# Modulation vectors in pairs over four blocks of partitions, their steps tied to the work around them, and the first head's gates by halves

## The chip, the cores and the metric

The kernel runs on one core of a Trainium2 chip. The core has a matrix engine (TensorE, PE in the profile; its weight loads are PEld), a vector engine (VectorE, DVE), an activation engine (ScalarE, ACT), a general engine (GpSimd, POOL) and a queue that here only issues DMAs (SyncE, SP). Each engine takes its instructions in order, and semaphores tie them together. The metric is the time of one execution on the device in microseconds (us). The runs before gave a median of 2446.35 us (three runs, 2445.74 to 2447.03).

## The reference

A trunk of two layers works on x (1 x 1024 x 1024, float32). Layer 0 mixes tokens with forgetting attention (16 heads of 64), layer 1 with gated linear attention (GLA, 4 heads, a recurrence over chunks); after each comes a SwiGLU channel mixer (hidden width 2816). Every sub-layer is normalised and modulated by six vectors that come from a conditioning vector c:

```python
c_act = jax.nn.silu(c)
for i in range(DEPTH):
    mod = c_act @ ada_w[i] + ada_b[i]              # 1024 x 6144 per layer
    sh1, sc1, g1, sh2, sc2, g2 = jnp.split(mod, N_MOD, axis=-1)
    h = modulate(rms_norm(x, norm1_g[i]), sh1, sc1)
    y = forgetting_attention(h, ...) if i % 2 == 0 else gated_linear_attention(h, ...)
    x = x + g1 * y
    h = modulate(rms_norm(x, norm2_g[i]), sh2, sc2)
    x = x + g2 * swiglu(h, ffn_w_in[i], ffn_w_out[i])
return rms_norm(x, final_g)
```

The gates of GLA are log_sigmoid of a low-rank projection, summed along the chunk: `b = cumsum(log_sigmoid(a @ w_a2 + b_a) / 16)`, and q and k are scaled by exp(b), exp(-b) and exp(b_last - b).

## The kernel before, in words

Activations lie transposed: 128 features by 1024 tokens per tile, in halves of 512 tokens. A product in float32 is made of three matmuls (`mm3`, L237 to L239) of operands that were split in a high and a low part: ACT writes the high part (L159, or L202 for weights), DVE or POOL the low part (L160, L205). SP loads the weights through a ring of three raw buffers (`wr`, `load_w`, L194).

The order of instructions on each engine is not simply the order in the program: a planner, which runs a model of the engines, picks the next instruction of each engine among those that it believes ready, earlier ones in the program first. It can move an instruction ahead of others where it believes its engine idle. `tc.issue_after(ins)` forbids it, for instructions of the same engine as `ins`, to come before `ins`; it adds no semaphore.

The stages on the chip are: loads, modulation vectors 0 and 1 of layer 0 and the first projections (to about 105 us); attention of layer 0 interleaved with the projections of the next pair of heads (`weave`; to about 640); the channel mixer of layer 0 (to about 1320); GLA (to about 1700); the channel mixer of layer 1 and the final norm.

A modulation vector is a matrix times a vector, and the kernel computes it without the matrix engine's streaming: 128 rows of `ada_w` are loaded at a time, multiplied by their eight values of silu(c) (`cact`, one value per partition) and added up in `acc`; at the end the 128 partitions are summed by matmuls with a column of ones, one per 128 columns (L377, tile `mp`), and the bias is added (L379, `modc`). `ada_steps` (L336) is a generator of such steps, and two paces, `ada0` and `ada1`, run it a step at a time beside other work:

- In attention (vectors 2 to 5 of layer 0) a step loads 128 x 1024 into a buffer of `wr` (`ada`, L345), and DVE does both operations in four instructions of 256 columns (L367, L369). Each projection of a pair of heads is worth three steps.
- In the channel mixer of layer 0 (vectors 0 and 1 of layer 1, `mid0`) and in GLA (vectors 2 to 5 of layer 1) a step loads 128 x 512 into one of three, in GLA of two buffers (`ad`, L345). ACT multiplies (L358 the first, L360 the others) and POOL adds (L361). `ADA_A` and `ADA_B` are what the two parts of a step cost the pace; every product of the mixer (`prod`) and every projection of GLA pays into it.

`ada0_mod` (L462 to L473), which makes vectors 0 and 1 of layer 0 at the start from tiles `adas` with its own `acc`, is not touched. `first_evac` ends the first projections.

In GLA the first head begins with `gv_body` (values, two blocks of 128 tokens each), `a_body` (the low-rank projection, one half of the tokens) and `gate_z` (L1596 to L1599). `gate_sum` (L1605 to L1610) does exp and ln on ACT, a subtraction and two scans on DVE, on tiles `b16` and `t2` (`b_s` and `t_s` in the rows). `gate_exps` (L1635 to L1642) makes all exponentials. `head_front` then projects K (`gk`) and Q (`gqp`), evacuates them with those exponentials, and steps `gate_ahead`, which makes the gates of the next head. `mp`, `gk`, `gqp`, `z` and `gv` share a ring of three PSUM banks (`pj`).

Of the kernel before, what the change touches and what calls it, by code (L numbers as in the profile page):

```python
# [9 lines left out]
F32 = mybir.dt.float32  # L10
# [4 lines left out]
ALU = mybir.AluOpType  # L15
# [38 lines left out]
def trunk(ctx, tc, x, c, ada_w, ada_b, norm1_g, norm2_g, ffn_w_in, ffn_w_out,  # L54
# [99 lines left out]
    nc.vector.memset(mhalf, -0.5)  # L154
    maskb = cst.tile([P, P], BF16, name="maskb")
# [130 lines left out]

    load_x(0)
# [28 lines left out]
    nc.scalar.activation(cact, vps[:, P:P + 8], AF.Silu)  # L316
    nc.vector.tensor_copy(vec, vps)
# [18 lines left out]
    def ada_steps(l, j, acc_of, raw_of, w):  # L336

        steps = deque((c0, k) for c0 in range(0, D, w) for k in range(8))
        got = deque()

        def load():
            if steps:
                c0, k = steps.popleft()
                raw = raw_of([P, w], F32, f"ada{l}{j}{c0}{k}")
                nc.sync.dma_start(raw, ada_w[l, psl(k), j * D + c0:j * D + c0 + w])  # L345
                got.append(raw)

        for c0 in range(0, D, w):
            acc = acc_of([P, w], F32, f"acc{l}{j}{c0}")
            for k in range(8):  # L350
                if w == D or c0 == k == 0:
                    load()
                raw = got.popleft()
                if w < D:
                    load()
                    yield ADA_A
                    if k == 0:
                        nc.scalar.mul(acc, raw, cact[:, 0:1])  # L358
                    else:
                        nc.scalar.mul(raw, raw, cact[:, k:k + 1])  # L360
                        nc.gpsimd.tensor_add(acc, acc, raw)  # L361
                    yield ADA_B
                    continue
                for q in range(0, w, 256):
                    cs = slice(q, q + 256)
                    if k == 0:
                        nc.vector.tensor_scalar(acc[:, cs], raw[:, cs], cact[:, 0:1], None, op0=ALU.mult)  # L367
                    else:
                        nc.vector.scalar_tensor_tensor(acc[:, cs], raw[:, cs], cact[:, k:k + 1], acc[:, cs],  # L369
                                                       op0=ALU.mult, op1=ALU.add)  # L370
                yield 1.0
            if w < D:
                yield ADA_B
            n, b = w // P, c0 // P
            mp = pj([P, n], F32, f"mp{l}{j}{c0}")
            for k in range(n):
                nc.tensor.matmul(mp[:, k:k + 1], acc[:, psl(k)], ones, start=True, stop=True)  # L377
            o = l * 48 + j * 8 + b
            nc.vector.tensor_add(modc[:, l, j, b:b + n], mp, vec[:, o:o + n])  # L379
            for i, jj in ((0, 1), (1, 4)):  # L380
                if j == jj:
                    make_a(l, i, slice(b, b + n))
        yield 1.0
# [25 lines left out]
    def ada1_queue(js, acc, raws_, w):  # L409
        r = Cycle(raws_)  # L410
        for j in js:
            ada1.q.append(ada_steps(1, j, lambda *_: acc, r, w))
# [441 lines left out]
    first_evac(1, acc)  # L854
    def v_half(g, half):
# [135 lines left out]
    for j in (2, 3, 4, 5):  # L991
        ada0.q.append(ada_steps(0, j, acc_r, wr, D))
# [523 lines left out]
    def mid0():  # L1516
        v = Views(slots["hid"], 2, [HALF], "ad0").v
        ada1_queue((0, 1), v[0], v[1:4], HALF)
# [24 lines left out]
    ada1_queue((2, 3, 4, 5), ada_v[0], ada_v[1:3], HALF)  # L1543
    ADA_A, ADA_B = 2.5, 1.0
# [57 lines left out]
    def gate_sum(h, bt):  # L1602

        b16, t2 = bt
        nc.scalar.activation(t2, t2, AF.Exp, scale=-1.0)  # L1605
# [311 lines left out]
```

## Time and profile before

| what | us |
|---|---|
| median of three runs | 2446.35 |
| the profiled execution | 2444.76 |
| its span, first to last instruction | 2443.0 |
| PE busy | 2384.9 |
| PEld busy | 2028.7 |
| DVE busy | 1703.0 |
| ACT busy | 1192.8 |
| POOL busy | 1151.1 |

The time of an execution is the span and 1.76 us around it. In the rows of the profile stand a line of the kernel, an engine, an operation, and what it writes and reads by the program's names; `x96` is a count. In lists of groups the next numbers are busy time in us, mean ns of one, and the idle time before it with what ended it. In lists of waits they are us in total, times, and the longest. In the timeline a row begins with the start and the duration in us, and square brackets hold the idle time of the engine before it and what ended it. Matmuls overlap, so a row of them lasts longer than the step to the next. PEclk is the clock granted to PE, as a share of full speed.

### The profile page before, as it was taken

The numbers are of one execution on the slowest core, as the hardware profiler recorded it, in microseconds if no ns is written. First come the engines' busy times: TensorE is split into PE (matmuls) and PEld (weight loads), VectorE is DVE, ScalarE is ACT, GpSimd is POOL, SyncE is SP. The second block draws the span as 40 slices with busy tenths as digits, with TensorE's granted clock in tenths as the row PEclk, the third lists the DMA queues.
The fourth block names the chain that finished last, engine by engine and source line by source line (L and its number), as shares of the span: only waits on it lengthen the run. The fifth ranks groups of instructions, "written<-read, shape, count | busy, mean of one in ns | idle before, by whom it ended". The sixth has DMA issues, their size and how long they took to land.

```text
span 2443.0 us, 35539 instructions
## 1 busy us (share of the span) xinstructions
PE 2384.9 (98%) x12458; PEld 2028.7 (83%) x12458; DVE 1703.0 (70%) x2849; ACT 1192.8 (49%) x2280; POOL 1151.1 (47%) x1006
## 2 busy tenths in 40 slices
PE   6999999999999999999999899999999999999998
PEld 5788888878887878888888798898888888888888
DVE  6477777776687768675788456546487667665787
ACT  4565665665554443435324756654344333335325
POOL 4233333333348776653363544442326656653362
PEclk9999999999999999999999999999999999999999
DMA  8224333233326544347665333435325434347664
GB/s 269 80 87 121 96 96 120 70 96 113 128 94 212 183 164 164 125 162 261 228 215 178 92 114 111 125 107 169 107 73 191 147 134 155 130 166 257 232 209 149
DMA packets 319067, 362.34 MB, mean 148 GB/s; under 512 B 18140, under 2 KB 246648, under 8 KB 318888
## 3 DMA queue, kind: packets, MB, share of 16 engines
q1 hardware_dynamic: 318888, 360.07, 44.2%
q8 instruction: 98, 1.61, 0.3%
q14 instruction: 81, 0.66, 0.1%
HBM read 269.76 MB, written 90.24 MB: 147 GB/s over the span
## 4 chain that ended last, share of the span: by engine, by line
PE 82%; DVE 7%; DMA 3%; ACT 3%; issue 3%; POOL 2%; SPq 0%; DVEq 0%; POOLq 0%; ACTq 0%
PE p_b L237 15%; PE p_b L239 15%; PE p_b L238 14%; PE o_b L947 2%; PE t_b L933 2%; PE qk_b L237 2%; PE qk_b L238 2%; PE qk_b L239 2%; DMA ad_s<-in_ada_w_dram 1%; PE s_b L902 1%; PE s_b L903 1%; PE gv_b L237 1%; PE gv_b L239 1%; PE gv_b L238 1%; PE vps_b L237 1%
## 5 line engine op out<-in xcount | busy, mean ns | idle before, releaser
L160 DVE TENSOR_TENSOR o_s<-xv_s,o_s 128x512 fp32r<-128x512 f32 (+1 forms) x376 | 325.8, 870 | 90.3 <-ACT o_s L159 89.0
L159 ACT CAST o_s<-xv_s 128x512 fp32r<-128x512 f32 (+1 forms) x376 | 217.3, 586 | 307.2 <-PE p_b L239 257.7
L237 PE MATMUL p_b<-B,o_s 128*128 128x512 f32 x608 | 236.9, 392 | 6.5 <-DVE x L1285 4.1
L238 PE MATMUL p_b<-B,o_s 128*128 128x512 f32 x608 | 238.1, 392 | 0.0
L239 PE MATMUL p_b<-B,o_s 128*128 128x512 f32 x608 | 237.5, 391 | 0.0
L913 POOL TENSOR_SCALAR lp_s<-lp_s,st 128x128 f32<-128x128 f32 (+7 forms) x128 | 96.2, 756 | 294.2 <-DVE st L912 280.8
L683 POOL TENSOR_TENSOR ex_s<-xv_s,xv_s 128x512 f32<-128x512 f32 (+1 forms) x64 | 89.3, 1396 | 254.2 <-DMA xv_s<-in_ffn_w_in_dram 92.1
L237 PE MATMUL p_b<-T,o_s 128*128 128x512 f32 x480 | 187.4, 391 | 0.0
L238 PE MATMUL p_b<-T,o_s 128*128 128x512 f32 x480 | 186.8, 389 | 0.0
L239 PE MATMUL p_b<-T,o_s 128*128 128x512 f32 x480 | 182.0, 389 | 0.0
L237 PEld LDWEIGHTS p_b<-B,o_s 128*128 128x128 f32 x608 | 114.9, 189 | 31.6 <-DVE x L1285 3.4
L239 PEld LDWEIGHTS p_b<-B,o_s 128*128 128x128 f32 x608 | 114.9, 189 | 24.0
L238 PEld LDWEIGHTS p_b<-B,o_s 128*128 128x128 f32 x608 | 114.9, 189 | 23.7
L911 ACT ACTIVATE lp_s<-lp_s,st 128x128 f32<-128x128 f32 (+7 forms) x128 | 99.3, 776 | 56.4 <-DVE st L907 55.9
L1285 DVE TENSOR_TENSOR ex_s<-ex_s,p_b 128x512 f32<-128x512 f32 x140 | 94.0, 681 | 34.6 <-PE p_b L239 34.3
L159 ACT CAST pt_s<-t_b 128x512 fp32r<-128x512 f32 (+1 forms) x160 | 80.1, 547 | 71.5 <-PE t_b L933 70.5
L685 POOL TENSOR_TENSOR xv_s<-ex_s,xv_s 128x512 f32<-128x512 f32 (+1 forms) x64 | 84.0, 1312 | 62.5 <-DVE o_s L160 60.4
L160 DVE TENSOR_TENSOR pt_s<-t_b,pt_s 128x512 fp32r<-128x512 f32 (+1 forms) x160 | 96.5, 631 | 18.2 <-ACT pt_s L159 17.5
L239 PEld LDWEIGHTS p_b<-T,o_s 128*128 128x128 f32 x480 | 90.1, 188 | 18.9
L238 PEld LDWEIGHTS p_b<-T,o_s 128*128 128x128 f32 x480 | 90.1, 188 | 18.5
L237 PEld LDWEIGHTS p_b<-T,o_s 128*128 128x128 f32 x480 | 90.1, 188 | 18.5
L907 DVE CUSTOM_DVE_ANT_0 lp_s<-s_b,cum_s 128x512 f32<-128x512 f32 (+3 forms) x128 | 72.7, 570 | 41.7 <-PE t_b L933 22.9
(1947 smaller groups left out, 7543.4 us busy)
## 6 DMA issues: line engine op xcount, KB each, us to landing
xv_s<-in_ffn_w_in_dram SPq DMA_DIRECT2D x176, 256.0 KB, 3.0
hid_B<-x SPq DMA_DIRECT2D x70, 512.0 KB, 2.6
ad_s<-in_ada_w_dram SPq DMA_DIRECT2D x96, 256.0 KB, 2.9
hid_T<-x SPq DMA_DIRECT2D x36, 512.0 KB, 2.7
xv_s<-in_ffn_w_out_dram SPq DMA_DIRECT2D x96, 192.0 KB, 4.6
ada_s<-in_ada_w_dram SPq DMA_DIRECT2D x32, 512.0 KB, 3.8
xv_s<-in_ffn_w_out_dram SPq DMA_DIRECT2D x40, 256.0 KB, 2.8
T2o<-hid_T SPq DMA_DIRECT2D x18, 512.0 KB, 8.5
```

The costliest lines, as they stand in the source:

```text
L159: nc.scalar.copy(hi, src)
L160: nc.vector.tensor_sub(lo, src, hi.bitcast(F32))
L237: nc.tensor.matmul(ps, ah, bh, start=start, stop=False)
L238: nc.tensor.matmul(ps, ah, bl, start=False, stop=False)
L239: nc.tensor.matmul(ps, al, bh, start=False, stop=stop)
L683: nc.gpsimd.tensor_add(s1, a21, a22)
L685: nc.gpsimd.tensor_sub(a11, s1, a11)
L907: nc.vector.tensor_tensor_reduce(lp[:, k0:k1], ps, cm[:, k0:k1], 1.0, mcur, ALU.add, ALU.min, mnew)
L911: nc.scalar.activation(lp, lp, AF.Exp, bias=mcur, scale=-1.0, accum_out=st[:, qi, 2:3])
L913: nc.gpsimd.tensor_scalar(lp, lp, st[:, qi, 3:4], 1.0, op0=ALU.mult, op1=ALU.mult)
L933: nc.tensor.transpose(tp[:, i, :], lps[qi][:, psl(2 * b + jj)], ident)
L1285: nc.vector.tensor_add(d, d if src is None else dest(G, src), ps)
```

## The change

Two vectors are made together. The 1024 rows of `ada_w` are taken as 32 groups r of 32 rows s. A step s loads row 32 r + s of each group r, over the 2048 columns of two vectors, with the columns cut in four blocks of 512: partition 32 q + r holds block q of group r. Each step is therefore still 128 x 512, but comes as four DMAs (32 partitions each), and `acc` is one tile of 512 columns for both vectors. In attention a buffer holds two steps. `cblk` holds silu(c) laid out for it (loaded four times, on ACT's queue, at the start), and `quart` has a 1 in column q for the partitions of block q, so that one matmul per 128 columns gives four sums. A pair has 32 steps of 128 x 512 (or 16 of two), as two vectors had before.

The DVE instructions of layer 0's steps may not come before the last DVE instruction of the first projections (`held`). The ACT multiplications of layer 1's steps may not come before the last ACT instruction written before them (`ADA_LAG` 0, in the channel mixer) or the seventh last (`ADA_LAG` 6, in GLA). In the first head of GLA sums and exponentials of the gates are made by halves of the tokens, the first half before the third value block, and the first head steps `gate_ahead` after its Q halves instead of its K halves.

```diff
+    quart = cst.tile([P, 4], F32, name="quart")
+    nc.vector.memset(quart, 0.0)
+    for q in range(4):
+        nc.vector.memset(quart[32 * q:32 * q + 32, q:q + 1], 1.0)
...
+    craw = mrows[4][:, 0:32]
+    cblk = cst.tile([P, 32], F32, name="cblk")
+    for q in range(4):
+        nc.scalar.dma_start(craw[32 * q:32 * q + 32], c[0].rearrange("(r s) -> r s", s=32))
...
+    nc.scalar.activation(cblk, craw, AF.Silu)
...
-    def ada_steps(l, j, acc_of, raw_of, w):
+    def last_of(e, n=0):
+        return [i for i in nc.cur_bb.bb.instructions[-400:] if i.engine == ENG[e]][-1 - n]
+
+    ADA_LAG = 0
+
+    def ada_pair(l, j, acc_of, raw_of, n):
+
+        steps = deque(range(0, 32, n))
+        got = deque()
+        rows_ = ada_w[l, :, j * D:(j + 2) * D].rearrange("(r s) (q m) -> q r s m", s=32, q=4)
 
         def load():
             if steps:
+                s = steps.popleft()
+                raw = raw_of([P, n * HALF], F32, f"ada{l}{j}{s}")
+                for q in range(4):
+                    nc.sync.dma_start(raw[32 * q:32 * q + 32].rearrange("r (s m) -> r s m", s=n),
+                                      rows_[q, :, s:s + n])
+                got.append((s, raw))
+
+        acc = acc_of([P, HALF], F32, f"acc{l}{j}")
+        for i in range(0, 32, n):
+            if n > 1 or i == 0:
+                load()
+            s0, raw = got.popleft()
+            if n == 1:
+                load()
+                yield ADA_A
+                with tc.issue_after(last_of("A", ADA_LAG)):
+                    if i == 0:
+                        nc.scalar.mul(acc, raw, cblk[:, 0:1])
                     else:
+                        nc.scalar.mul(raw, raw, cblk[:, i:i + 1])
+                if i:
+                    nc.gpsimd.tensor_add(acc, acc, raw)
                 yield ADA_B
+                continue
+            tie = held[0]
+            for s in range(s0, s0 + n):
+                for c0 in range(0, HALF, 256):
+                    cs, rs_ = slice(c0, c0 + 256), slice((s - s0) * HALF + c0, (s - s0) * HALF + c0 + 256)
+                    with tc.issue_after(tie):
+                        if s == 0:
+                            nc.vector.tensor_scalar(acc[:, cs], raw[:, rs_], cblk[:, 0:1], None, op0=ALU.mult)
+                        else:
+                            nc.vector.scalar_tensor_tensor(acc[:, cs], raw[:, rs_], cblk[:, s:s + 1], acc[:, cs],
+                                                           op0=ALU.mult, op1=ALU.add)
+            yield 1.0
+        if n == 1:
+            yield ADA_B
+        mp = pj([P, 16], F32, f"mp{l}{j}")
+        for b in range(4):
+            nc.tensor.matmul(mp[:, b:16:4], acc[:, psl(b)], quart, start=True, stop=True)
+        o = l * 48 + j * 8
+        nc.vector.tensor_add(modc[:, l, j:j + 2, :].rearrange("p j k -> p (j k)"), mp, vec[:, o:o + 16])
+        if j in (0, 4):
+            make_a(l, j // 4)
         yield 1.0
...
     first_evac(1, acc)
+    held = [last_of("D")]
...
-    for j in (2, 3, 4, 5):
-        ada0.q.append(ada_steps(0, j, acc_r, wr, D))
+    for j in (2, 4):
+        ada0.q.append(ada_pair(0, j, acc_r, wr, 2))
...
-        ada1_queue((0, 1), v[0], v[1:4], HALF)
+        ada1_queue((0,), v[0], v[1:4])
...
-    ada1_queue((2, 3, 4, 5), ada_v[0], ada_v[1:3], HALF)
-    ADA_A, ADA_B = 2.5, 1.0
+    ada1_queue((2, 4), ada_v[0], ada_v[1:3])
+    ADA_A, ADA_B, ADA_LAG = 2.5, 1.0, 6
...
-    def gate_sum(h, bt):
+    def gate_sum(h, bt, halves=(0, 1)):
 
         b16, t2 = bt
...
+        w = slice(halves[0] * HALF, (halves[-1] + 1) * HALF)
+        nc.scalar.activation(t2[:, w], t2[:, w], AF.Exp, scale=-1.0)
+        nc.scalar.activation(t2[:, w], t2[:, w], AF.Ln, bias=1.0)
+        nc.vector.tensor_sub(t2[:, w], b16[:, w], t2[:, w])
+        for hf in halves:
...
-    def gate_exps(h, bt):
+    def gate_exps(h, bt, halves=(0, 1), to=None):
...
-            next(ahead, None)
+            if h:
+                next(ahead, None)
         wq = feed.next()
...
+            if not h:
+                next(ahead, None)
         return kin, qt
...
+    to0 = sm.tile([P, 4, NB], F32, tag="dec", name="dec0"), Tr([P, S], F32, "ei0")
+    gate_sum(0, bt, (0,))
+    gate_exps(0, bt, (0,), to0)
     vt.append(gv_body(0, wv, 2))
     a_body(aw, 1, bt)
     gate_z(0, (1,), bt)
-    gate_sum(0, bt)
-    b16, t2, ei, dec = gate_exps(0, bt)
+    gate_sum(0, bt, (1,))
+    b16, t2, ei, dec = gate_exps(0, bt, (1,), to0)
     vt.append(gv_body(0, wv, 3))
```

More of the change, by code (lines that the diff above doesn't have):

```diff
@@ L341, in load @@
         def load():
             if steps:
[L343 to L358, printed above, removed]
-                    else:
[L360 to L372, printed above, removed]
-                yield ADA_B
[L374 to L382, printed above, removed]
```

27 lines of the change are left out of this document (13 added, 14 removed).

## The prediction

> **What bounds the kernel now.** I read the page's totals first, then the list of what PE waited for, then busy time by stretch, and last the order of instructions where PE stands still. On the page:
>
> ```profile
> span 2443.0 us, 35539 instructions
> PE 2384.9 (98%) x12458; PEld 2028.7 (83%) x12458; DVE 1703.0 (70%) x2849; ACT 1192.8 (49%) x2280; POOL 1151.1 (47%) x1006
> PE 82%; DVE 7%; DMA 3%; ACT 3%; issue 3%; POOL 2%; SPq 0%; DVEq 0%; POOLq 0%; ACTq 0%
> ```
>
> PE is busy all but 58.1 us, and the chain that ended last is PE for 82%. So only two things shorten this kernel: fewer TensorE instructions, or fewer of those 58.1 us. The waits of PE and the busy time by stretch (columns: stretch, its length, then PE, PEld, DVE, ACT and POOL busy, granted clock, DMA) say where they lie:
>
> ```profile
> PE mp_b L472 <- DVE acc L470: 6.6, 2, 5.3
> PE gk_b L237 <- DVE modc L379: 4.6, 1, 4.6
> 63.30:68.80 5.50, 4.63 (x18) 3.94 (x19) 2.35 (x7) 3.96 (x7) 2.27 (x3) 0.50 0.72 223
> 1388.90:1393.20 4.30, 4.30 (x10) 3.43 (x11) 2.17 (x6) 4.18 (x15) 0.00 (x0) 0.50 0.00 1
> 711.00:1240.00 529.00, 522.49 (x2317) 431.98 (x2316) 381.72 (x484) 224.19 (x397) 325.82 (x224) 1.00 0.55 193
> 1824.00:2330.00 506.00, 506.00 (x2234) 419.00 (x2233) 353.93 (x464) 201.56 (x356) 272.45 (x189) 1.00 0.51 178
> ```
>
> A stall is paid twice: after each of the two long ones PE works on at granted clock 0.50. The channel mixer of layer 0, which carries modulation steps of layer 1, loses 6.5 us of PE; that of layer 1, without them, loses none.
>
> **The change part by part.**
>
> *Matmuls removed.* One modulation vector needed 8 matmuls with the accumulator as weights; a pair of vectors now needs 4.
>
> ```profile
> L377 PE MATMUL mp_b<-ones,ad_s 128*128 128x1 f32 x96 | 11.7, 233 | 0.0
> L377 PE MATMUL mp_b<-ones,acc_s 128*128 128x1 f32 x64 | 8.2, 236 | 0.0
> 753.07 0.39 PE L239 MATMUL p_b<-B,o_s 128*128 128x512 f32 x1
> 753.30 0.50 PE L377 MATMUL mp_b<-ones,ad_s 128*128 128x1 f32 x4
> 753.66 0.49 PE L237 MATMUL p_b<-T,o_s 128*128 128x512 f32 x1
> 753.99 0.40 PE L238 MATMUL p_b<-T,o_s 128*128 128x512 f32 x1
> ```
>
> The trace shows two records for each of these f32 matmuls: 160 for 10 vectors of 8. After it 5 pairs of 4 leave 40, so 120 go. By busy time a record is 19.9/160 = 0.124 us, 14.9 in all. By what they push away: from 753.30 to 753.99 are 0.69 us, of which the ordinary step of 0.23 (753.07 to 753.30) belongs to the next matmul; 0.46 for 4 records is 0.115 each, 13.8 in all; without the change-over, 0.36/4 = 0.09, 10.8. PE has no idle time there to absorb it. I take the middle, **-13.0** (-10.8 to -14.9). Four moving columns instead of one, and one addition of 16 columns on DVE instead of two of 8 or four of 4, I cost at nothing: the first is beside a full weight load, the second off the path; were that cover gone, the fewer additions would still be a gain.
>
> *Held back at first.* Layer 0's first accumulation steps now may not pass the last DVE instruction of the first projections. DVE, then PE, today:
>
> ```profile
> 56.57 1.21 DVE L367 TENSOR_SCALAR acc_s<-ada_s,cact 128x256 f32<-128x256 f32 x1
> 57.70 1.33 DVE L470 SCALAR_TENSOR_TENSOR acc<-adas_s,cact,acc 128x256 f32<-128x256 f32 x1
> 58.95 3.20 DVE L367 TENSOR_SCALAR acc_s<-ada_s,cact 128x256 f32<-128x256 f32 x3
> 62.07 0.68 DVE L484 TENSOR_TENSOR h0l<-y_s,h0h 128x512 fp32r<-128x512 f32 x1
> 63.29 0.98 PE L472 MATMUL mp_b<-ones,acc 128*128 128x1 f32 x4 [5.28 <-DVE acc L470]
> ```
>
> Four instructions of L367, whose vectors only the output projection after attention needs, stand ahead of the last two L470 (one at 57.70, one behind 62.07) that PE waits for: 1.13 + 3.12 = 4.25 us of start-to-start time. They go; a neighbour may get slower, so -3.8. Then the half clock: 5.5 us at 0.50 cost 2.75, of which I take half, -1.4, since about 1.5 us of stall stay. Sum **-5.2** (-3.0 to -7.0). The Trainium skill, "TensorE: Matmul & The Clock Gate", Part 1, says that the rate is set by whole windows of about 3.4 us; the two 0.50 rows above agree that the slow time outlasts the stall. By that rule a stall well under a window would give back all 2.75, and the sum would be 1.35 lower.
>
> What the hold costs: the steps keep their buffers longer, and SP, in order, waits with the next weight loads for them.
>
> ```profile
> 64.76 0.38 SPq L194 DMA_DIRECT2D wv_s<-in_fox_w_in_dram  x1
> 105.94 4.93 POOL L205 TENSOR_TENSOR wv_0l_s<-wv_s,wv_0h_s 128x256 fp32r<-128x256 f32 x3 [12.88 <-ACT wv_0h_s L202]
> 121.14 0.28 PE L237 MATMUL vps_b<-wv_0h_s,h0h 128*128 128x256 f32 x1
> ```
>
> The weights are split 41 us after their issue and used by PE at 121, so most of the delay is slack; 0 to +5, nearer 0: **+1.0**. The 16 postponed DVE instructions then run beside attention, where DVE has room.
>
> *First head's gates by halves.* Today, ACT, then DVE, then PE (another table load, as long, stands between the two):
>
> ```profile
> 1379.47 1.28 ACT L1605 ACT_TABLE_LOAD   x1
> 1380.77 1.06 ACT L1605 ACTIVATE t_s<-t_s 128x1024 f32<-128x1024 f32 x1
> ...
> 1383.14 1.06 ACT L1606 ACTIVATE t_s<-t_s 128x1024 f32<-128x1024 f32 x1
> 1384.23 1.23 DVE L1607 TENSOR_TENSOR t_s<-b_s,t_s 128x1024 f32<-128x1024 f32 x1 [3.77 <-ACT t_s L1606]
> 1385.49 3.28 DVE L1610 TENSOR_TENSOR_SCAN b_s<-ad_s,t_s 128x512 f32<-128x512 f32 x2
> 1388.88 0.79 PE L237 MATMUL gk_b<-h1h,w_h_s 128*128 128x512 f32 x1 [4.62 <-DVE modc L379]
> ```
>
> PE's 4.6 us end at 1388.88, when DVE has evacuated `mp`, which sat behind that chain on DVE and held the bank PE wanted. Two causes go: there are 2 `mp` instead of 8 in this stage, none after the first K projection, and half of the chain is done earlier (half of 1.06 twice, of 1.23 and of 3.28: 3.3 us). `next(ahead)` of the first head moves behind its Q projections, so its `z` no longer takes a bank between the K projections. Price: the first half adds about two table loads, 2 x 1.28 = 2.6 us, to an ACT that waits in this stretch. -4.6, and the half clock of 1388.90:1393.20, 4.3/2 = 2.1: **-6.7** (0 if another evacuation takes its place, -6.7 at best; nearest the row itself).
>
> *Steps tied.* An ACT multiplication of a step may no longer be moved ahead of the ACT work written before it (six instructions of grace in the recurrence). Today it is moved ahead and then waits for its DMA, with weight splits queued behind it:
>
> ```profile
> ACT ad_s L360 <- DMA ad_s<-in_ada_w_dram: 83.7, 55, 5.6
> SPq L345 <- POOL ad_s L361: 135.0, 71, 9.0
> L345 SPq DMA_DIRECT2D ad_s<-in_ada_w_dram x96: 327/328/532, 709.9 to 1649.8; - x96
> L361 POOL TENSOR_TENSOR ad_s<-ad_s,ad_s x51: 1277/1298/2212, 719.0 to 1654.1; 128x512 f32<-128x512 f32 x51
> L360 ACT ACTIVATE ad_s<-ad_s,cact x84: 707/724/729, 717.6 to 1653.0; 128x512 f32<-128x512 f32 x84
> DMA to landing us min/median/max: 2.6/2.9/5.7
> ```
>
> It can return the 6.5 us of 711 to 1240, or move them: behind a later multiplication wait POOL's addition, POOL's weight sums, and SP's next load. +3 to -6.5; I take **-2.5**, under half. The additions become 93 instead of 84: 9 x 1.30 = 11.7 us of POOL, hidden by its idle 203 us of 711:1240 and by the recurrence.
>
> *Quarter loads.* A step's 256 KB come as 4 issues, so 288 more in layer 1 and, by the same count, 96 in layer 0: 384 x 0.328 = 126 us of SP. SP is on the ending chain with 0%, and a load is issued a step ahead of its use; I cost it at **0** (-0 to +126: the rival below). A step lands about 3 x 0.33 = 1.0 us later.
>
> *At the start* four small loads on ACT's queue, a second Silu and five small fills. On SP such an issue took 0.36, so 1.4 us; ACT waited 2.09 us for x:
>
> ```profile
> 1.24 0.36 SPq L290 DMA_DIRECT2D mrows_s<-in_c_dram  x1
> ...
> 4.17 1.06 ACT L439 ACTIVATE sq_s<-xt_s 128x1024 bf16<-128x1024 f32 x1 [2.09 <-DMA xt_s<-in_x_dram]
> 4.88 0.28 PE L312 MATMUL vps_b<-ident,mrows_s 32*128 32x32 f32 x1 [4.88 <-DMA mrows_s<-in_final_g_dram]
> ```
>
> Hidden, but they share the DMA engines with x: 0 to +1.4, **+0.4**.
>
> Sum: -13.0 - 5.2 + 1.0 - 6.7 - 2.5 + 0 + 0.4 = -26.0. The profiled execution took 2444.76 us (span 2443.0 and 1.76 around it), so 2418.8; the median shown, 2446.35, is 1.6 above it: **2420**.
>
> **The rivals.**
>
> *The stalls come back elsewhere.* An order made anew puts new short waits where the old ones were; only the matmuls go: 2446.35 - 13.0 = 2433. For it: the planner moved those instructions ahead because it believed DMA and POOL faster than they are, and it still will. Against: both long stalls have one named instruction that the change takes out of the way.
>
> *It does nothing measurable.* If PE's time between those matmuls were set by others, the 13 us would turn into waiting: 2446. Against: idle 0.0 in both L377 rows.
>
> *Slower: SP's queue.* SP issues in order, and 135 us of it already wait at L345 for POOL's additions; behind the four issues stand the weight loads of the mixers and of the recurrence. Each step takes SP 3 x 0.328 = 0.98 us longer. All passed on to PE would be +126, that is 2546; it decides from 26/126 = 21% of it, and at half of it the time is 2420 + 63 = 2483. Against: the same POOL waits leave PE only 6.5 us idle in 529, so weights come well ahead.
>
> *Slower: quarters land one after the other.* Four landings of 2.9 us are 11.6; with the multiplication 0.72 and the addition 1.30, over two buffers, 6.8 us a step in the recurrence against the 4.8 us that its 64 steps now take (1341 to 1650): 64 x 2.0 = 128, about 2548. Against: four small loads issued from 1.24 on had all landed when PE started at 4.88. The Trainium skill, "DMA: Bandwidth & Descriptors", Rules for kernel authors, speaks against the change here: it advises one 128-partition transfer, because parts serialize on the same 16 engines, and calls transfers below 64 KB mostly overhead. No run shows quarters of this kind yet.
>
> **How the numbers follow.** Forecast 0.52 (own range 2411 to 2428); stalls come back 0.26 (2428 to 2441); nothing 0.07; SP's queue 0.12; serial quarters 0.03. Within 0.2%, about 4.9 us, counts as no change, the least that a measurement of this kernel can tell. Faster 0.52 + 0.26 = 0.78, same 0.07, slower 0.15. The range 2410 to 2446 takes in the forecast with its bounds, the first rival, and half of no change; outside are the slower cases and a little.
>
> **What would show it.** Right: 40 records of `mp` for layers 0 (16) and 1 (24) instead of 160; the wait of L472 under 2 us and the granted clock back to 1.00 before 66; no wait of `gk_b` on `modc`; less ACT waiting for `ad_s` and PE idle under 4 us in the first mixer. Wrong: a wait of PE of several us on weights (`DVE w_l_s`, `o_s`) near 115 or in the recurrence, with SP before it at the quarter loads; or `ad_s` landing after 6 us or more.

## The result and the profile after

The changed kernel took 2429.78 us (median; 2426.91 to 2435.19), the kernel before 2446.69 beside it: a ratio of 0.9934 with the 95% interval 0.9916 to 0.9952, 16 us (12 to 21) faster. 2420 was predicted, with 2410 to 2446 as the range: the sign and the range held, but the middle was 10 us too low, and the time lies above the forecast's own range of 2411 to 2428. The profiled execution took 2430.71 us. The first page of its profile, totals and chain of waits:

```profile
span 2429.0 us, 36104 instructions
PE 2375.2 (98%) x12338; PEld 2019.5 (83%) x12338; DVE 1689.5 (70%) x2845; ACT 1192.6 (49%) x2286; POOL 1164.0 (48%) x1015
PE 78%; DVE 6%; DMA 6%; ACT 3%; issue 2%; POOL 2%; SPq 2%; DVEq 0%; POOLq 0%; ACTq 0%
```

PE stays the bound, and SP is now on the ending chain with 2%. PE's idle time is the span less its busy time, 53.8 us; before it was 58.1. The matmuls of the modulation vectors of both layers, in the view of the tile `mp` (count, shortest, median and longest in ns, first and last start):

```profile
L397 PE MATMUL mp_b<-quart,ad_s x24: 167/252/253, 1032.6 to 1648.7; 128*128 128x4 f32 x24
L397 PE MATMUL mp_b<-quart,acc_s x16: 167/252/253, 281.8 to 436.4; 128*128 128x4 f32 x16
```

They are 40 records, 120 fewer, as counted. If the removed matmuls brought what the prediction says, 13 us, everything else together brought only 3 of the 13 us it was to bring. Where they went is seen by stage. The table gives the length of each stage in us, from the start of one matmul to that of another, in one profile of each kernel. Single profiles differ by a few us from run to run: in four profiles of kernels whose code for attention is that of the changed kernel, the third stage takes 524.0, 522.8, 520.4 and 520.3 us.

| stage (from, to) | before | after | predicted change |
|---|---|---|---|
| start to the last forget-gate matmul | 96.4 | 89.4 | -4.8 (hold -5.2, start +0.4) |
| from there to the first q and k matmul | 10.4 | 14.3 | 0 |
| from there to the last output of attention | 520.8 | 524.0 | -5.2 (48 records), +1.0 (cost of the hold) |
| first mixer (from its first sum of squares, `sp`, to its first output matmul, `f0e`) | 629.5 | 618.8 | -2.6 (24 records) and most of the ties' -2.5 |
| GLA (from `f0e` to the last output of GLA, `go`) | 412.7 | 409.5 | -5.2 (48 records) and -6.7 |

The first mixer gained 10.7 us, twice what it was to gain; attention and GLA got little or nothing. The waits of PE that matter, in the list of what PE waited for:

```profile
PE mp_b L481 <- DMA adas_s<-in_ada_w_dram: 7.2, 2, 5.3
PE vps_b L320 <- DMA mrows_s<-in_final_g_dram: 7.1, 1, 7.1
PE o_b L968 <- DVE pt_s L164: 4.2, 6, 1.3
PE qk_b L241 <- DVE v_s L164: 3.2, 1, 3.2
PE s_b L923 <- DVE st L928: 3.1, 2, 2.7
PE gqp_b L241 <- DVE gy_s L1699: 2.0, 1, 2.0
```

The two long stalls of before (`mp` waiting for the accumulation, `gk` for `modc`) are gone. Two new ones stand in attention, one of 3.2 and one of 2.7 us, and short ones there (`o_b`) have grown from 2.0 to 4.2 us. The same in busy time by stretch:

```profile
62.30:67.80 5.50, 4.30 (x28) 3.59 (x29) 2.20 (x5) 1.88 (x4) 4.48 (x5) 1.00 0.16 47
102.40:109.20 6.80, 5.54 (x13) 4.42 (x14) 4.94 (x14) 1.39 (x3) 0.33 (x1) 0.50 0.66 190
300.40:307.20 6.80, 5.58 (x22) 4.99 (x23) 4.00 (x15) 2.26 (x6) 0.80 (x1) 0.50 0.52 162
711.00:1240.00 529.00, 529.00 (x2339) 438.21 (x2338) 394.74 (x492) 225.01 (x400) 338.60 (x232) 1.00 0.59 197
```

Near 65 us the granted clock is 1.00 where it was 0.50, and in the mixer's stretch PE is idle 0.0 of 529 us, where it was 6.5. But the clock is at 0.50 for 6.8 us at 102 and again at 300. PE is busy 5.5 us in each of these stretches, so half clock costs about 2.8 us each time, on top of 5.9 us of waits.

How the first of the two came about is read from the order on DVE, and then PE's row, in the timeline:

```profile
98.90 0.47 DVE L390 SCALAR_TENSOR_TENSOR acc_s<-ada_s,cblk,acc_s 128x256 f32<-128x256 f32 x1
99.40 0.42 DVE L164 TENSOR_TENSOR v_s<-vps_b,v_s 128x256 fp32r<-128x256 f32 x1
99.74 0.47 DVE L390 SCALAR_TENSOR_TENSOR acc_s<-ada_s,cblk,acc_s 128x256 f32<-128x256 f32 x1
100.13 2.27 DVE L805 TENSOR_TENSOR_SCAN cum_s<-zt_s 16x1024 f32<-16x1024 f32 x1
102.33 0.84 DVE L390 SCALAR_TENSOR_TENSOR acc_s<-ada_s,cblk,acc_s 128x256 f32<-128x256 f32 x2
103.10 0.74 DVE L164 TENSOR_TENSOR v_s<-vps_b,v_s 128x256 fp32r<-128x256 f32 x2
...
103.66 0.77 PE L241 MATMUL qk_b<-h0h,w_h_s 128*128 128x512 f32 x1 [3.18 <-DVE v_s L164]
```

The steps that were held back (L390) come free behind the first projections, and DVE takes them there, in the midst of the cumulative sum and of the copies of v out of PSUM. The bank of q and k comes free late by them, and by the scan of 2.3 us (without such steps at this place a wait of 1.6 us is left, below). The second, near 300 us, begins with a step that is taken early, finds its quarter load not there, and has scores' work behind it. From 295.2 us on DVE works without a gap until PE's wait ends, with three more pairs of step instructions (0.9 us each) between the scores' work:

```profile
291.05 1.72 SPq L361 DMA_DIRECT2D ada_s<-in_ada_w_dram  x4
295.23 0.88 DVE L390 SCALAR_TENSOR_TENSOR acc_s<-ada_s,cblk,acc_s 128x256 f32<-128x256 f32 x2 [2.03 <-DMA ada_s<-in_ada_w_dram]
301.62 0.48 PE L923 MATMUL s_b<-KA,QA 128*128 128x128 f32 x1 [2.68 <-DVE st L928]
```

The loads of layer 1, in the view of their tile `ad`:

```profile
L361 SPq DMA_DIRECT2D ad_s<-in_ada_w_dram x384: 310/419/1690, 710.1 to 1637.6; - x192
DMA to landing us min/median/max: 1.8/2.0/4.7
```

And what ACT waited for them, 55.5 us in place of 83.7 and half as often, in the list of waits:

```profile
ACT ad_s L377 <- DMA ad_s<-in_ada_w_dram: 55.5, 28, 5.4
```

### The profile page after: what moved, and what is told of

It is laid out like the page before. It is cut to its first block, busy times and chain, and to the rows that moved or that the text cites. A ratio compares the mean times of both kernels' runs of the same rounds, so it can differ in the third digit from the quotient of the medians.

```text
span 2429.0 us, 36104 instructions
## 1 busy us (share of the span) xinstructions
PE 2375.2 (98%) x12338; PEld 2019.5 (83%) x12338; DVE 1689.5 (70%) x2845; ACT 1192.6 (49%) x2286; POOL 1164.0 (48%) x1015
## 4 chain that ended last, share of the span: by engine, by line
PE 78%; DVE 6%; DMA 6%; ACT 3%; issue 2%; POOL 2%; SPq 2%; DVEq 0%; POOLq 0%; ACTq 0%
PE p_b L241 16%; PE p_b L243 16%; PE p_b L242 16%; PE o_b L968 2%; PE t_b L954 2%; SPq L361 1%; DMA ad_s<-in_ada_w_dram 1%; PE qk_b L241 1%; PE qk_b L242 1%; PE qk_b L243 1%; DMA ada_s<-in_ada_w_dram 1%; PE s_b L923 1%; PE s_b L924 1%; PE vps_b L241 1%; PE vps_b L242 1%
## 5 line engine op out<-in xcount | busy, mean ns | idle before, releaser
L164 DVE TENSOR_TENSOR o_s<-xv_s,o_s 128x512 fp32r<-128x512 f32 (+1 forms) x376 | 333.4, 890 | 82.3 <-ACT o_s L163 81.3
L242 PEld LDWEIGHTS p_b<-T,o_s 128*128 128x128 f32 x480 | 90.1, 188 | 18.6
L968 PE MATMUL o_b<-pt_s,v_s 128*128 128x256 f32 x512 | 95.6, 295 | 5.9 <-DVE pt_s L164 4.2
```

The costliest lines, as they stand in the source:

```text
L164: nc.vector.tensor_sub(lo, src, hi.bitcast(F32))
L242: nc.tensor.matmul(ps, ah, bl, start=False, stop=False)
L968: nc.tensor.matmul(ops, lv, pts[b][:, hl, 2 * jj:2 * jj + 2, :], start=j == 0 and hl == 0, stop=False)
```

## The experiments

My theory after the result: the matmuls brought their 13 us; the ties brought far more than was predicted, since without them the pairs would be slower than the kernel before; and the hold and the pairs' steps in attention lost again what the first projections had gained. The rivals were that the tie does little and the loads little harm, or that the matmuls were worth less and the stalls moved less. Ratios are to the kernel before, which took 2444.6 to 2445.5 us beside them (2446.69 beside the changed kernel).

| kernel | median us | ratio | 95% interval |
|---|---|---|---|
| changed | 2429.78 | 0.9934 | 0.9916 to 0.9952 |
| without the hold | 2431.93 | 0.9951 | 0.9939 to 0.9963 |
| without the ties | 2463.75 | 1.0077 | 1.0063 to 1.0090 |
| gates by halves alone | 2439.93 | 0.9983 | 0.9974 to 0.9992 |
| without gates by halves | 2430.69 | 0.9948 | 0.9935 to 0.9960 |
| before, with quarter loads | 2449.46 | 1.0016 | 1.0006 to 1.0027 |
| before, with the ties | 2437.43 | 0.9973 | 0.9962 to 0.9983 |
| changed, matmuls four times | 2442.87 | 0.9989 | 0.9977 to 1.0002 |
| changed, hold behind v | 2428.19 | 0.9933 | 0.9920 to 0.9947 |
| changed, attention tied | 2455.30 | 1.0037 | 1.0022 to 1.0051 |
| changed, loads of c moved in the program | 2429.12 | 0.9936 | 0.9923 to 0.9949 |
| changed, hold behind v and c on SP | 2428.22 | 0.9924 | 0.9912 to 0.9937 |
| the same, attention tied loosely | 2429.53 | 0.9932 | 0.9918 to 0.9946 |

**Without the hold**

```diff
-                    with tc.issue_after(tie):
-                        if s == 0:
...
+                    if s == 0:
...
```

> The changed kernel without the hold on layer 0's steps. Theory A (the hold only moves a stall): without it DVE again stands between the last acc and PE near 58 to 63 us, the first projections end near 96 us instead of 89, but the 3.2 us wait of qk_b on v_s near 104 us and the half clock behind it (2.7 us) are gone; the time is within 3 us of the changed kernel, about 2431. Theory B (the hold is worth what I predicted, 5.2 us, and the stall near 104 us has another cause): the wait near 104 us stays and the time is about 2435 to 2437.

It was 2431.93 us. The first projections end at 97.6 us, as late as before the change (96.4), and PE's wait for v is shorter, though not gone:

```profile
PE s_b L922 <- DVE st L927: 3.0, 2, 2.7
PE qk_b L241 <- DVE v_s L164: 1.7, 1, 1.7
```

The stage to the last forget-gate matmul is 8.2 us longer than with the hold, the whole kernel only 2 us by the medians (4 by the ratios, with intervals that overlap). At the first q and k matmul it is still 6.6 us behind (110.3 against 103.7), at the last output of attention only 1.7 us (629.4 against 627.7). So most of what the hold gains at 65 us is given back in attention: 519.1 us without the hold, 520.3 to 524.0 in the four profiles with it. What gives it back there isn't shown.

**Without the ties**

```diff
-                with tc.issue_after(last_of("A", ADA_LAG)):
-                    if i == 0:
...
+                if i == 0:
...
```

> The changed kernel without the tie of layer 1's ACT multiplications. Theory A (the tie took PE's stalls out of the first channel mixer): PE idle in 711 to 1240 us is back at 4 to 7 us (it is 0 with the tie) and the time is 2434 to 2438. Theory B (pairs alone did it, by other places of the steps): PE idle in the mixer stays below 1.5 us and the time is within 3 us of 2430.

It was 2463.75 us, 34 us above the changed kernel and 19 above the kernel before, far more than either theory had. The stretch of the mixer in the view of busy time by stretch:

```profile
711.00:1240.00 529.00, 514.06 (x2242) 422.67 (x2241) 368.62 (x466) 220.30 (x388) 320.99 (x220) 0.99 0.55 186
```

What ACT waited for:

```profile
ACT ad_s L376 <- DMA ad_s<-in_ada_w_dram: 88.2, 52, 4.2
```

One of the stalls in the timeline (ACT twice, DVE, PE):

```profile
741.58 0.72 ACT L376 ACTIVATE ad_s<-ad_s,cblk 128x512 f32<-128x512 f32 x1 [3.54 <-DMA ad_s<-in_ada_w_dram]
742.21 0.60 ACT L163 CAST o_s<-xv_s 128x512 fp32r<-128x512 f32 x1
742.84 1.40 DVE L164 TENSOR_TENSOR o_s<-xv_s,o_s 128x512 fp32r<-128x512 f32 x1 [3.03 <-ACT o_s L163]
744.90 0.79 PE L241 MATMUL p_b<-B,o_s 128*128 128x512 f32 x1 [5.28 <-DVE x L1305]
```

These four rows show what the tie prevents: an ACT multiplication that was moved ahead waits 3.54 us for its load, a split stands behind it on ACT, DVE waits 3.03 us for the split, and PE 5.28 us for DVE. PE is idle 14.9 of 529 us, against 0.0 with the tie. The first mixer takes 641.8 us (618.8 with the tie) and GLA 422.4 (409.5): the two stages that lost their ties are 23 and 13 us longer, which is the loss of the whole kernel.

**The gates by halves, alone and left out.** In the first, the kernel before gets only the halves of `gate_sum` and `gate_exps` and the later step of `gate_ahead`; in the second, the changed kernel has them whole again. Of the first:

```diff
...
+    gate_sum(0, bt, (0,))
+    gate_exps(0, bt, (0,), to0)
     vt.append(gv_body(0, wv, 2))
...
```

> The kernel before with the gates by halves and the later look-ahead of the first head alone. Theory A (prediction: the stall of gk_b on modc goes, 4.6 us and 2.1 us of half clock): 2440 to 2441. Theory B (the gates make new waits in the same place, gr_b on gvt and gqp_b on gy as in the changed kernel, and the clock falls for a window all the same): 2444 to 2447.

> The changed kernel with the first head's gates whole, as before. Theory A (the gates by halves are worth 6.7 us): about 2436. Theory B (with pairs no mp stands in the first head any more, so the stall goes without the halves): within 3 us of 2430, and no wait of gk_b over 1.5 us near 1375 us.

Alone they bring 4.2 us (1 - 0.9983, times 2445; 2 to 6 by the interval), near theory A of the first. Within the changed kernel they bring 1 us by the medians and 3 by the ratios, whose intervals overlap, as theory B of the second said. There, without them, the wait stands at another matmul, since `modc` no longer lies behind the chain. PE's list of waits without the halves:

```profile
PE gqp_b L241 <- DVE b16a_s L1620: 4.7, 1, 4.7
```

And two rows of DVE in its timeline:

```profile
1383.72 1.23 DVE L1628 TENSOR_TENSOR t2a_s<-b16a_s,t2a_s 128x1024 f32<-128x1024 f32 x1 [4.95 <-ACT t2a_s L1627]
1385.46 2.34 DVE L1631 TENSOR_TENSOR_SCAN b16a_s<-ad_s,t2a_s 128x512 f32<-128x512 f32 x2
```

Here the chain belongs to the next head's gates, which `gate_ahead` starts between the K halves. With the halves and the later step, a wait of `gqp` of 2.0 us for the evacuation of Q is left (above).

**The split of the loads alone.** The kernel before, with each load cut in four of 32 partitions:

```diff
-                nc.sync.dma_start(raw, ada_w[l, psl(k), j * D + c0:j * D + c0 + w])
+                for q in range(4):
+                    qs_ = slice(32 * q, 32 * q + 32)
+                    nc.sync.dma_start(raw[qs_], ada_w[l, k * P + 32 * q:k * P + 32 * q + 32, j * D + c0:j * D + c0 + w])
```

> The kernel before, with each load of a modulation vector's weights in the attention, the mixer and the recurrence cut into four loads of 32 partitions; matmuls, steps and their order stay as before. Theory A: the loss of the changed kernel without its ties (18.6 us over the kernel before, though it has 120 matmul records less) comes from the split loads, which land later or in another order and let the steps of the mixer slip: then this kernel is slower than before, 2455 to 2472 us, with PE idle of over 10 us between 711 and 1240 us (6.5 before). Theory B: it comes from the new order of the steps (32 short ones for a pair of vectors in place of 8 for each half), not from the loads: then this kernel is within 5 us of before, 2441 to 2450 us.

It cost 3.9 us (1 to 7): little, and what theory B allows. Its quarters are 32 rows that lie side by side, those of the pairs every 32nd row, but in both kernels they land in 2.0 us (median). So the 18.6 us of the untied pairs are not the loads by themselves. What is left is the order that the planner makes of the pairs' steps; why it is worse for 32 steps in one accumulator than for four times 8 is not shown by a run.

**The ties alone.** The kernel before, with `issue_after` on its own multiplications:

```diff
+                    with tc.issue_after(last_of("A", ADA_LAG)):
                         if k == 0:
                             nc.scalar.mul(acc, raw, cact[:, 0:1])
...
```

> The kernel before with nothing but the ties: each multiply of ACT for a modulation vector of layer 1 is issued behind the last ACT instruction written ahead of it in the mixer, and behind the seventh last in the recurrence; vectors one by one, loads and matmuls as before. Theory A: the ties put right what any untied set of steps loses, in the kernel before too: PE idle between 711 and 1240 us falls from 6.5 to under 2, and the time to 2436 to 2441 us. Theory B: the ties only repair what the pairs break: the time stays within 3 us of before, 2442 to 2449 us. Prediction's price of the ties alone: 2.5 us, 2442.6 us.

It was 2437.43 us: 6.6 us faster than before, where 2.5 were predicted. In the stretch of the mixer:

```profile
711.00:1240.00 529.00, 528.56 (x2348) 438.03 (x2347) 394.24 (x488) 223.73 (x396) 331.72 (x229) 1.00 0.56 196
```

PE is idle 0.4 us of 529. The first mixer takes 621.5 us in place of 629.5. So the old steps were hurt by the same lead over their loads, only less. In this one profile GLA is 4.5 us longer than before (417.2); the 6.6 us are what is left of all stages.

**The matmuls four times.** The changed kernel with as many records as before:

```diff
         for b in range(4):
-            nc.tensor.matmul(mp[:, b:16:4], acc[:, psl(b)], quart, start=True, stop=True)
+            for _ in range(4):
+                nc.tensor.matmul(mp[:, b:16:4], acc[:, psl(b)], quart, start=True, stop=True)
```

> The changed kernel with each of its 20 matmuls against the block columns done four times over, 160 records in place of 40, as many as the kernel before has. If the records that the change took away were worth their own duration on the path (the prediction's 0.108 us each, 13.0 us in all), this is 13 us slower than the changed kernel, 2441 to 2445 us. If four back to back cost less than the ones spread over eight columns, or part of them lies in waits, it is 4 to 8 us slower, 2434 to 2438 us.

```profile
L398 PE MATMUL mp_b<-quart,ad_s x96: 167/253/356, 1029.4 to 1661.2; 128*128 128x4 f32 x96
L398 PE MATMUL mp_b<-quart,acc_s x64: 167/252/253, 280.9 to 439.3; 128*128 128x4 f32 x64
```

The 120 records more cost 13.1 us by the medians, 13.4 by the ratios (8 to 19 by the intervals). Divided by 120 that is 0.11 us each, but the stages don't share it so. The row of the mixer in the timeline, first in the changed kernel, then here, and the stretch behind it here:

```profile
1032.60 0.95 PE L397 MATMUL mp_b<-quart,ad_s 128*128 128x4 f32 x8
1033.41 0.49 PE L242 MATMUL p_b<-B,o_s 128*128 128x512 f32 x1
...
1029.38 3.97 PE L398 MATMUL mp_b<-quart,ad_s 128*128 128x4 f32 x32
1033.21 0.77 PE L242 MATMUL p_b<-B,o_s 128*128 128x512 f32 x1
...
1032.50:1039.30 6.80, 6.80 (x19) 5.47 (x19) 4.89 (x6) 2.01 (x4) 3.72 (x3) 0.50 0.77 272
```

8 records hold PE for 0.81 us, 32 for 3.83, which is 0.13 us for each of the 24 more. But behind the 32 PE goes on at half clock for 6.8 us, without having waited, which costs up to another 3.4 us. The first mixer takes 626.3 us in place of 618.8. GLA, with 48 records more, takes 415.8 in place of 409.5. Attention also has 48 more, and takes 521.2 us from the first q and k matmul, no more than the four profiles without them (520.3 to 524.0). There PE's idle time shrinks instead, from 8.3 to 5.0 us (changed kernel first):

```profile
104.00:520.00 416.00, 407.69 (x2625) 357.65 (x2625) 307.78 (x824) 250.12 (x545) 155.26 (x213) 0.99 0.33 101
104.00:520.00 416.00, 411.05 (x2682) 362.40 (x2681) 309.18 (x827) 251.51 (x546) 154.96 (x213) 0.99 0.33 101
```

**The hold behind v.** The instruction behind which the first steps are held is taken after the copies of v were written:

```diff
-    held = [last_of("D")]
...
     run(v_half(0, 1))
+    held = [last_of("D")]
```

> The changed kernel, with the instruction behind which the first steps are held taken after the second half of v has been built, so that these steps come behind the copies of v too. Theory A: the hold only moved the stall, and the held steps that stood behind the cumulative sums' inputs delayed the copies of v: the wait of 3.2 us of the query and key matmuls for the split of v near 104 us and the half clock behind it go, 2424 to 2427 us. Theory B: something else is late there (the wait passes to the cumulative sums or to the loads): within 2 us of the changed kernel, 2428 to 2432 us.

It was 2428.19 us, within 2 us of the changed kernel, as theory B said. PE's wait for v falls from 3.2 to 1.6 us, but its waits for `st` rise from 3.1 us in two to 7.0 us in four, so the gain at the first place is lost again behind it.

**Attention tied.** Each DVE instruction of a step stands behind the third last DVE instruction written ahead of it:

```diff
-            tie = held[0]
+            tie = last_of("D", 2)
```

> The changed kernel, with the steps of layer 0 in attention tied as those of layer 1 are: each DVE instruction of a step may not come before the third last DVE instruction written ahead of its step, in place of the one hold behind the first projections. Theory A: attention lost its share of the matmuls' gain (it takes 538.3 us from the last forget-gate matmul to the last output of attention, 531.2 before) because its steps are as untied as those of the mixer were without their tie, are moved ahead and then hold DVE while they wait for a load (18.2 us in 14 waits): then the waits of PE for the split of v (3.2 us) and for the scores' exponent input st (2.7 us) go, attention takes 527 to 532 us, and the time is 2420 to 2425 us. Theory B: attention is longer for another reason (the half clock of windows that fall by chance, more DMAs): it stays over 535 us and the time within 2 us of the changed kernel, 2428 to 2432 us; or the ties make scores wait for steps, and it is slower.

This theory fell: the kernel took 2455.3 us, and attention 563.5 us from the last forget-gate matmul in place of 538.3. No step waits for its load any more, but the steps now keep their buffers, which are those of the weights. SP's waits, this kernel first and then the changed one:

```profile
SPq L198 <- DVE acc_s L390: 120.4, 15, 25.2
```

```profile
SPq L198 <- DVE acc_s L390: 24.1, 12, 3.0
```

SP stands 120 us with weight loads behind steps that have not freed their buffer, and in the stretch from 104 to 520 us PE is idle 25.4 us (8.3 in the changed kernel). That this wait is the whole of the loss isn't shown, but the looser tie below takes both away together. In the mixer and in GLA the steps have buffers of their own, and there the tie is free of this.

**The start.** In the first of two, the four loads of c were moved in the program but stayed on ACT's queue; in the second SP issues them behind the first projections' weights, with the hold behind v; there `cblk` is also made later. Of the second:

```diff
...
     load_ada0(2)
+    for q in range(4):
+        nc.sync.dma_start(craw[32 * q:32 * q + 32], c[0].rearrange("(r s) -> r s", s=32))
...
```

> The changed kernel with the four loads of c for the block layout issued behind the first weight loads on ACT's queue, not ahead of the first x. Theory A: at the start they share the DMA engines with the rows that PE's first matmul waits for (final_g, 7.1 us in place of 4.9): then that wait is back at about 5 us, the first projections end 1.4 to 2 us sooner (87.5 to 88 us in place of 89.4), and the time is 2427.5 to 2429 us. Theory B: the delay at the start is hidden behind the x and weight loads of the next microseconds: the first projections end within 0.5 us of 89.4, and the time is that of the changed kernel.

> The changed kernel with the hold behind the second half of v, as in hold_later, and the four loads of c for the block layout issued by SP behind the first projections' weights, not by ACT as the first four loads of all. Theory A: SP issues a load only when the eighth load before it, on either queue, has landed (in the changed kernel its third small load waits 1.5 us for a load of c); without four loads of c among the first, PE's first matmul waits about 5 us again in place of 7.1, the first projections end at 87 to 88 us in place of 88.9, and the time is 1 to 2 us below hold_later's 2428.2: 2425.5 to 2427.5 us. Theory B: x and the first weights set the end of that stage whatever PE's first wait is: within 0.7 us of hold_later at the end of the first projections, and in the time.

The first moved nothing: ACT's queue has no other work so early, and issues them at 0.80 us all the same (its timeline):

```profile
0.80 1.83 ACTq L317 DMA_DIRECT2D mrows_s<-in_c_dram  x4
```

So it is a repetition of the changed kernel, and its 2429.12 us agree. Its profile has the same two waits of PE in attention to the hundredth, 3.18 us for v and 2.68 for `st`. But in the two stretches around them, which the changed kernel spent at 0.50, the mean clock is 0.75, that is half of the time at 0.50:

```profile
102.40:109.20 6.80, 5.88 (x20) 4.76 (x21) 5.08 (x14) 2.80 (x4) 1.94 (x3) 0.75 0.77 218
300.40:307.20 6.80, 6.42 (x31) 5.47 (x32) 3.84 (x15) 2.38 (x7) 2.00 (x4) 0.75 0.49 156
```

Its attention takes 520.3 us from the first q and k matmul, and 534.5 from the last forget-gate matmul. So the 3.2 us by which attention looked longer than before are within what one and the same code varies; what stays is that it didn't get shorter.

In the second SP no longer waits for c (in the changed kernel its list of waits, below, shows 1.5 us), and PE's first wait falls from 7.1 to 6.2 us:

```profile
SPq L300 <- DMA mrows_s<-in_c_dram: 1.5, 1, 1.5
```

```profile
PE s_b L921 <- DVE st L926: 7.1, 3, 4.0
PE vps_b L320 <- DMA mrows_s<-in_final_g_dram: 6.2, 1, 6.2
```

The first projections end at 89.3 us (88.9 with the hold behind v alone): what is late in the first 15 us is hidden behind the loads of x and the weights, as theory B said.

**Attention tied loosely**, on top of that kernel:

```diff
-            tie = held[0]
+            tie = last_of("D", 40) if s0 else held[0]
```

> The same kernel, with the steps of attention tied loosely: each DVE instruction of a step not before the 41st last DVE instruction written ahead of its step (some 20 us of its work), where attn_tie had the third last. Theory A: attn_tie lost 25 us because the steps kept their buffers, which are those of the weights, and SP waited 120 us with weights behind them; a loose tie leaves the buffers time and still forbids the worst of the waits for loads: SP waits under 50 us for the steps at its weight loads, attention takes 528 to 534 us, and the time is 2420 to 2426 us. Theory B: any tie in attention costs more by the buffers than it saves by the waits: attention is longer than without it (over 538 us) and the time over 2428 us.

With 2429.53 us it is not told from the kernel without it, 2428.22. SP's waits at the weight loads for steps fall from 33.8 to 21.8 us and DVE's waits for step loads from 19.9 (15) to 13.0 (7), but attention takes 536.4 us from the last forget-gate matmul, not 534 or less. The four profiles of the changed kernel's attention have 534.5 to 538.3, so no effect of the loose tie on attention can be told. No version here is told from the changed kernel as faster: the best ratio, 0.9924, has an interval that overlaps its own.

## Why the prediction came out as it did

**Matmuls (-13.0): right in count and in total, not place by place.** There are 40 records in place of 160, and putting 120 back cost 13.4 us. That this is so near 13.0 is in part luck: it holds up to 3.4 us of half clock behind a row of 32 records in the mixer, and in the mixer of the kernel before no such stretch stands behind its rows of 4. In attention the 48 records put back cost nothing that can be seen, and taking them away shortened it by nothing either. The step between neighbours, 0.09 to 0.115 us, was read at one place in the mixer and carried over to attention. That PE was idle for 0.0 us before the rows of `mp` says only that it didn't wait right there; from 104 to 520 us it waited 6.9 us before the change and 8.3 after. So the 5.2 us that the sum gave to attention were not there to be had.

**Held back (-5.2, cost +1.0): the gain right at its place, its cost mis-sized and sought in the wrong place.** What was to show it did: the wait of `mp` for the accumulation (L491 now) fell from 6.6 to 0.5 us, the granted clock near 65 us is 1.00, and the stage ends 7.0 us sooner. The Trainium skill, "TensorE: Matmul & The Clock Gate", Part 1, ties half clock to whole windows of activity; the trace agrees here, a wait of 0.5 us left no half clock. But the whole kernel without the hold lost only 2 to 4 us. The cost was looked for in the weights' buffers and on SP; SP did stand behind held steps, once for 29.7 us, but no long wait of PE for weights came of it. A part lay on DVE: the held steps were released together beside the cumulative sum and the copies of v, and PE's wait there is 3.2 us in place of 1.7. (The way from the forget gate to the first q and k matmul is 3.9 us longer than before, but 2.3 of these are there without the hold too.) The rest goes in attention, and what takes it there stays open. The question that the prediction didn't ask is what stands on the same engine at the place where a held instruction comes free.

**Gates by halves (-6.7): mis-sized.** The wait of `gk` on `modc` is gone, as forecast. Alone they brought 4.2 us, in the changed kernel between 1 and 3, where the fewer `mp` have already taken `modc` out of the chain: with the pairs and whole gates the wait has left `gk` and stands at `gqp`. The prediction gave all of it to the gates, though it named both causes.

**Ties (-2.5): mis-sized most.** Alone they brought 6.6 us. The prediction took under half of the 6.5 us that PE waited in the mixer; all of them went, and the stage got 8.0 us shorter, with its half clock. In the changed kernel they are worth 34 us, because the pairs without them are 18.6 us slower than the kernel before, fewer matmuls and all. This was a condition of the forecast that the prediction took as given.

**Quarter loads (0): 3.9 us, alone.** The rivals "SP's queue" and "quarters land one after the other" did not come: a quarter landed in 2.0 us (median) after its issue, where the whole load took 2.9, and the four of 291.05 were in use by 295.23. Issues took 0.42 us each in place of 0.33, so a step takes SP 1.35 us more, more than the 0.98 reckoned. The Trainium skill, "DMA: Bandwidth & Descriptors", Rules for kernel authors, advises against such a split, since parts run on the same engines; the measured loss has its sign, but is 3% of the 128 us that landing one after another would have cost. SP's queue came true only where attention was tied.

**Start (+0.4):** PE's first matmul of the accumulation came 1.4 us later (14.3 in place of 12.9), and nothing of it reached the end of the stage.

**The sum.** -26 was forecast and -16 came. Against the forecast's terms the gates lack some 4 us, the hold 1, the loads 4, and the ties give 4 more (each by its own run). That leaves about 5 of the 10 us, with an uncertainty of several us, since each run's interval reaches 2 to 4 us to either side. It is the size of the 5.2 us of matmuls in attention, which took 520.3 to 524.0 us with the change and 520.8 before. By its time, what happened is the rival "the stalls come back elsewhere" (2428 to 2441), which had half the chance of the forecast. By its places it is half of that rival: two stalls came in attention, where the planner took the new steps ahead of their loads as it had the old ones, but both long stalls and those of the mixer went. Why attention gives back what the hold gains stays open; a later hold, the loads of c and ties were each tried there, and none brought it back.

## What to carry to other kernels

A step that fills idle time on an engine must not be taken before its data is there, and what cured it here is an order tied to the work around it; but only where its buffers were its own, else the tie kept buffers that the main work waited for. An instruction that is held back comes free somewhere: read what stands on its engine there before counting the gain. Price a removed matmul by the step between its neighbours only in the stages where PE never waits, and when you put matmuls back to confirm it, read every stage: the total can agree for another reason.

## What the runs showed of the hardware

- Half clock doesn't follow the length of the stall. Waits of 3.18 and 2.68 us each came with 6.8 us at 0.50 in the changed kernel and with 3.4 us in its repetition; one of 5.28 us (no ties) came with 3.4 us (0.51 from 744.8 to 748.2 us, 1.00 after). At 300 us the clock was already down from 300.4, before the wait ended at 301.62. The Trainium skill, "TensorE: Matmul & The Clock Gate", Part 1, has windows of 3413 ns that run freely, which agrees with lengths of 3.4 and 6.8 us; that an idle window of that length is needed isn't what is seen, as a wait of 2.68 us was enough.
- Half clock came without any wait, too: with the matmuls four times, behind a row of 32 small matmuls (4 moving columns, 3.83 us) the clock was 0.50 for 6.8 us, in which PE was busy all the time.
- A load of 32 partitions took SP 0.42 us to issue, one of 128 partitions and four times the bytes 0.33.
- The wait of SP at 2.4 us in the changed kernel was for the landing of a 4 KB load of c, and with ACT's four loads of c behind the first weights that wait was gone. So four small loads on another queue delayed SP's by 1.5 us. The waiting load is the ninth issued, counted over both queues; the first two are a load of c from ACT and one of x from SP, and the tenth waits 0.4 us for x. That an issue waits for the eighth load before it fits this count, but no run shows that it is the reason.
